# Projecting queries, keys and values of the second layer in blocks of 512 columns instead of 384

## The chip, the cores and the metric

The kernel runs on one core of one Trainium2 chip. Its time is the device time of one execution in microseconds, given as the median of a few runs. Five engines work side by side, each through its own list of instructions in order: TensorE (PE in the profile, with its weight loads as PEld), VectorE (DVE), ScalarE (ACT), GpSimd (POOL) and SyncE (SP), which issues nearly all of this kernel's transfers. Semaphores tie the lists together. Matmul results go to PSUM, from where DVE and ACT read them.

## The reference

Two layers work on 512 tokens of width 1024 with 16 heads of 64. Each layer does

```
hn = rms_norm(x, gain);  y = mixer(hn);  x = x + y
```

Layer A (dilated attention) projects to three groups of queries, keys and values and to a gate. Layer B (neighbourhood attention on a grid of 8 rows and 64 columns) is the one that the change touches:

```
proj = hn @ w_in                       # 1024 x 4096: q, k, v, gate
q = rms_norm(q per head, q_gain) / 8;  k = rms_norm(k per head, k_gain)
logits = q . k + bias(row, column),  masked to a window of 16 columns
y = softmax(logits) @ v * silu(gate);  return y @ w_out
```

All inputs and outputs are 32-bit floats.

## The kernel before

**Matmuls.** Each float is split into a rounded high part and a rest (`split`, line 124: ACT rounds at line 128, DVE or, two times in five, GpSimd subtracts at line 134). A product is then three matmuls: high by high, high by low, low by high (`mm3`, line 215). All matmuls are issued in `matmul` at line 209, all transposes on TensorE at line 213, so the profile tells them apart by their tiles: `acc<-` are projections and output products, `log` scores, `o` the weighted sum of values, `tp` transposes.

**Weights.** The weights lie in memory in the order in which they are used. `blocks` (line 137) lists the blocks, `loads` cuts them into transfers of at most 1024 columns, `raws` keeps three of those in flight in SBUF, and `splits` (line 186) splits pieces of 384 or 512 columns and runs three pieces ahead of the matmuls (line 192). `kernel`'s helper `_layout` packs the weights on the host in the same order.

**Layer B** works on eight pairs of heads, called `hc` 0 to 7. For each pair `main_b` (line 1000) does two things on TensorE:

- `project_qk(384, 4, "raw", hc, ...)`: queries, keys and values of the pair, 128 columns each. For each of eight slices of the width (`k`) and each of four groups of 128 tokens (`i`), one `mm3` with the normalised tokens as the stationary operand and 384 weight columns as the moving one, into four accumulators (`project`, line 245). After the last slice each accumulator is evacuated by ACT (line 477) into a part of the tile `rk`, and `squares` (line 278) forms the sums of squares of queries and keys: four heads' worth, GpSimd at line 284, DVE at line 285.
- `project_t`: the gate's 128 columns, now with the weights stationary and all 512 tokens moving, 24 matmuls. DVE multiplies the result by the token scale (line 1007), ACT takes the tanh, and DVE ends the SiLU later.

`head_norm` (line 291) turns the sums into factors with a Newton iteration for the inverse square root (`rsqrt`, line 105; on GpSimd it has 14 operations, on DVE 11) and multiplies them in on DVE (line 307). In layer B the multiplication is held back until the pair's gate has been scaled (`later`, line 1008).

**The attention of a pair** is `side_b` (line 1015): transposes of queries and keys, scores in two halves (`scores`), softmax on DVE and ACT, and the turning of the probabilities. For pairs 0 to 5 these are turned by DVE into the tile `tr` and sent through memory (`turner`, line 733: a write `td<-tr`, four reads `pt<-td`), and the weighted sum (`weigh`, line 1098) follows later. Pairs 6 and 7 turn them on TensorE. `put_y` (line 674) multiplies by the gate and splits the result for the output product.

**The order of the work.** The order on TensorE is written out by hand. `run` (line 906) walks through the main generator (projections, output product) and, in between, pulls steps from the side generator (the attentions) whenever its due time has come. Time here is a clock that the program itself keeps while it issues matmuls (line 207: 213 ns for a moving operand of 512 columns). `yield "wait", ("raw", hc), 12000` means: go on when 12 us of that clock have passed since block `hc` was projected. `later_on` sets a timer on the same clock. A guard such as `("qk", hc - 1)` makes the main generator pull side steps until that stamp exists. On the other engines a scheduler places the instructions by estimated times, except where `keep_in_program_order` fixes them.

The bias of a pair is loaded by `bias_b` (line 718) into one of two tiles; the gate tiles are three, the accumulators four, the side banks of PSUM four.

Of the kernel before, what the change touches and what calls it, by code (L numbers as in the profile page):

```python
# [13 lines left out]
F32 = mybir.dt.float32  # L14
# [8 lines left out]
P = 128  # L23
S = 512
D = 1024
DH = 64
NHC = 8
KT = 8
# [5 lines left out]
A_HC = 1280 * KT  # L34
A_OUT = A_HC * NHC
B_IN = A_OUT + KT * D
B_HC = 512 * KT
B_OUT = B_IN + B_HC * NHC
W_COLS = B_OUT + KT * D


@with_exitstack
def tile_hybrid_encoder(
# [93 lines left out]
    def blocks():  # L137

        for hc in range(NHC):
            b = hc * A_HC  # L140
            first = hc == NHC - 1
            yield from ((b + 512 * KT * (i ^ first), 512, KT) for i in range(2))
            if hc == NHC - 1:
                yield b - A_HC + 1152 * KT, 128, KT
            yield b + 1024 * KT, 128, KT
            if hc != NHC - 2:
                yield b + 1152 * KT, 128, KT
        yield from outs(A_OUT)
        for hc in range(NHC):
            b = B_IN + hc * B_HC  # L150
            yield from ((b, 384, KT), (b + 384 * KT, 128, KT))
        yield from outs(B_OUT)

    def outs(b):
# [133 lines left out]

    later = []

    def head_norm(raw, ss, ns, held, delay=0):


        rs = wk.tile([P, 32], F32, tag="rs", name="rs")
        rsqrt(nc.vector if ns == 8 else nc.gpsimd, rs[:, : 4 * ns], ss[:, : 4 * ns], 4 * ns, 1.0 / DH)

        def scale():
            for i in range(4):
                by = rs[:, i * ns : (i + 1) * ns].unsqueeze(2)
# [142 lines left out]
    def part(n):  # L442
        return rk[:, 1024 * n : 1024 * n + 1024].rearrange("p (i c) -> p i c", i=4)

    def project_qk(n, ns, key, hc, guard, first=False, **kw):

        box = []

        def evac(i, acc):
            if not box:  # L450
                if key == "rawq":
                    t = wk.tile([P, 4 * n], F32, tag="rawq", name=key, bufs=1)
                    box.append(
                        t.rearrange("p (c i r) -> p c i r", c=16, i=4)
                        if moved(hc)
                        else t.rearrange("p (i c) -> p i c", i=4)
                    )
                elif key == "rawk":
                    box.append(part(0))
                    st["v12", hc] = part(1 + hc % 3)  # L460
                else:
                    o = 4 * n * (hc % 3)
                    box.append(rk[:, o : o + 4 * n].rearrange("p (i c) -> p i c", i=4))
                box.append(wk.tile([P, 32], F32, tag="ss", name="ss"))
            raw, ss = box
            if key == "rawq" and moved(hc):
                src = acc.rearrange("p (f a r) -> p f a r", f=4, a=4)
                pieces = [(raw[:, :, i, :].rearrange("p (a f) r -> p f a r", a=4), src)]
            elif key == "rawk":
                pieces = [(raw[:, i, :], acc[:, :256]), (st["v12", hc][:, i, :], acc[:, 256:])]  # L470
            else:
                pieces = [(raw[:, i, :], acc[:, :n])]
            for dst, src in pieces:
                if first:
                    nc.scalar.copy(dst, src)
                else:
                    nc.scalar.activation(dst, src, AF.Copy, scale=rs_n[:, i : i + 1])  # L477
            if not first:
                squares(raw[:, :, i, :] if key == "rawq" and moved(hc) else raw[:, i, : ns * 64], ss, i, ns)

        tile_of = lambda hn: lambda k, i: hn[:, k, P * i : P * (i + 1)]
        yield from project(tile_of(hn_h), tile_of(hn_l), n, evac, guard, **kw)
        raw, ss = box
        if first:
            st["first"] = raw, ss
            return
        normed(raw, ss, ns, key, hc)

    def normed(raw, ss, ns, key, hc):
        head_norm(raw, ss, ns, key == "raw", 9000 if key == "rawk" and 0 < hc < NHC - 1 else 0)  # L490
        if key == "rawq" and moved(hc):
            turn_q(raw)
        st[key, hc] = raw
        stamp[key, hc] = clock[0]
# [502 lines left out]
        nc.vector.tensor_add(xk, xk, acc)  # L997
        nc.sync.dma_start(out[P * f : P * f + P, :], xk)

    def main_b(hc):  # L1000
        yield from project_qk(384, 4, "raw", hc, ("qk", hc - 1) if hc else ("rs", "b"))
        acc = []
        yield from project_t(acc)
        yield ("yb", hc - 3, "y") if hc else ("rs", "all")
        gt = wk.tile([P, S], F32, tag="gt", name="gt", bufs=3)
        eg = wk.tile([P, S], F32, tag="eg", name="eg")
        tc.keep_in_program_order(nc.vector.tensor_mul(gt, acc[0], rs_half))
        while later:
            later.pop()()
        nc.scalar.activation(eg, gt, AF.Tanh)  # L1010
        gated(hc, gt, eg)
# [2 lines left out]

    def side_b(hc):
        if hc >= 2 and far(hc - 2):
            yield "wait", ("raw", hc), 1500
            pending.pop(0)()
            yield
        if hc >= 1 and far(hc - 1):  # L1020
            if hc + 1 < NHC:
                st["e", hc + 1] = bias_b(hc + 1)
        yield "wait", ("raw", hc), 12000 if hc < NHC - 1 else 11000
        raw = st.pop(("raw", hc))
        e = st.pop(("e", hc))
        qh = wk.tile([P, 512], F32R, tag="q0h", name="qh", bufs=1)
# [70 lines left out]

        def weigh():
            assert not any(t.left for t in turners)
            o = bank("o")  # L1100
            mms = []


            for d, n, m, i, a in (
# [5 lines left out]
                if n == 256:  # L1110
                    q, p = [[P, 2]] + q, [[32, 2]] + p
                mms.append((
                    lambda t_, d=d, q=q: sb(t_, d, q),
                    lambda hs, m=m: raw[:, m, 256 + hs.start : 256 + hs.stop],
                    lambda hd, p=p, i=i, a=a: sb(pt, at(a, hd, i), p),
                ))
            side_by_side(o, mms)
# [22 lines left out]
    def main():  # L1140
# [5 lines left out]
        gap[0] = cycle((500, 500, 800))  # L1146
        for hc in range(2):
            st["e", hc] = bias_b(hc)
        for hc in range(NHC):
            yield from main_b(hc)  # L1150
        yield from out_product("yb", sink_b)

    def side():
# [83 lines left out]
def _layout(x, norm_gain, a_w_in, a_w_out, a_q_gain, a_k_gain, t5_bias,  # L1237
# [20 lines left out]
        parts.append(cols(wa, [c(0, 2)]))  # L1258
        parts.append(cols(wa, [9 * D + P * hc]))
    parts += outs(wao)  # L1260
    for hc in range(NHC):
        parts.append(cols(wb, [i * D + P * hc for i in range(3)]))
        parts.append(cols(wb, [3 * D + P * hc]))
    parts += outs(wbo)
    w = np.concatenate(parts, axis=1)

# [32 lines left out]
```

## Time and profile before

| what | value |
|---|---|
| runs of the kernel, median (lowest to highest) | 851.97 us (850.87 to 852.74), 3 runs |
| the profiled execution, its own time | 852.44 us |
| its span in the trace | 850.6 us |
| instructions | 15397 |
| granted TensorE clock, mean | 0.999 |
| memory read / written | 109.11 MB / 31.12 MB |

In the rows of the profile, a group's row has line, engine, operation, tiles, shapes and count, then its total busy time and the mean of one in ns, then the idle time ahead of it and what ended it. A row of the timeline begins with start and duration in us. A row of stretches has the busy time of each engine between two times. A row of waits says who waited for whom: total us, times, longest. Layer B's first projection starts at 577 us, its output product at about 793 us.

### The profile page before, as it was taken

The numbers are of one execution on the slowest core, as the hardware profiler recorded it, in microseconds if no ns is written. First come the engines' busy times: TensorE is split into PE (matmuls) and PEld (weight loads), VectorE is DVE, ScalarE is ACT, GpSimd is POOL, SyncE is SP. The second block draws the span as 40 slices with busy tenths as digits, with TensorE's granted clock in tenths as the row PEclk, the third lists the DMA queues.
The fourth block names the chain that finished last, engine by engine and source line by source line (L and its number), as shares of the span: only waits on it lengthen the run. The fifth ranks groups of instructions, "written<-read, shape, count | busy, mean of one in ns | idle before, by whom it ended". The sixth has DMA issues, their size and how long they took to land.

```text
span 850.6 us, 15397 instructions
## 1 busy us (share of the span) xinstructions
PE 842.8 (99%) x5546; PEld 702.5 (83%) x5546; DVE 518.5 (61%) x1336; ACT 431.5 (51%) x923; POOL 309.8 (36%) x494
## 2 busy tenths in 40 slices
PE   9999999999999999999999999999999999999998
PEld 7788878788788788788788787789998898889786
DVE  7354684684674674674675745447567656766642
ACT  7433653653653653652653554355366655665531
POOL 2252441542541541542531341121354335542511
PEclk9999999999999999999999999999999999999999
DMA  7346377477478378378375562264245664555333
GB/s 250 110 126 216 97 228 227 137 226 241 128 227 248 102 228 243 102 230 246 99 236 159 147 191 79 60 241 146 82 143 138 174 175 148 168 163 158 99 97 127
DMA packets 65228, 141.23 MB, mean 166 GB/s; under 512 B 5760, under 2 KB 23104, under 8 KB 65152
## 3 DMA queue, kind: packets, MB, share of 16 engines
q1 hardware_dynamic: 65008, 139.99, 54.5%
q8 instruction: 44, 0.72, 0.3%
q10 hardware_dynamic: 144, 0.26, 0.1%
q14 instruction: 32, 0.26, 0.1%
HBM read 109.11 MB, written 31.12 MB: 165 GB/s over the span
## 4 chain that ended last, share of the span: by engine, by line
PE 94%; ACT 3%; DVE 1%; DMA 1%; issue 0%; DVEq 0%; ACTq 0%
PE acc L209 80%; PE log L209 5%; PE o L209 5%; PE tp L213 3%; ACT p L1084 1%; ACT p L672 1%; DMA x_all<-in_xt 0%; ACT p L831 0%; ACT wh L128 0%; DVE hn_l L397 0%; ACT rawk L477 0%; DMA eb<-lb_d 0%; PE pa L209 0%; PE pl L209 0%; DVE p L820 0%
## 5 line engine op out<-in xcount | busy, mean ns | idle before, releaser
L128 ACT CAST wh<-wraw 128x512 fp32r<-128x512 f32 (+1 forms) x275 | 161.4, 588 | 294.7 <-PE acc L209 258.0
L209 PE MATMUL acc<-wh,hn_h 128*128 128x512 f32 (+1 forms) x768 | 293.8, 383 | 1.6 <-ACT rawq L477 0.8
L209 PE MATMUL acc<-wh,hn_l 128*128 128x512 f32 (+1 forms) x768 | 285.6, 373 | 0.0
L209 PE MATMUL acc<-wl,hn_h 128*128 128x512 f32 (+1 forms) x768 | 285.5, 373 | 0.0
L134 POOL TENSOR_TENSOR wl<-wraw,wh 128x512 fp32r<-128x512 f32 (+1 forms) x110 | 136.9, 1244 | 361.0 <-ACT wh L128 341.7
L134 DVE TENSOR_TENSOR wl<-wraw,wh 128x512 fp32r<-128x512 f32 (+1 forms) x166 | 111.1, 670 | 141.5 <-ACT wh L128 137.0
L209 PEld LDWEIGHTS acc<-wh,hn_h 128*128 128x128 f32 x768 | 144.6, 188 | 29.2 <-issue 4.9
L209 PEld LDWEIGHTS acc<-wh,hn_l 128*128 128x128 f32 x768 | 144.5, 188 | 20.8
L209 PEld LDWEIGHTS acc<-wl,hn_h 128*128 128x128 f32 x768 | 145.0, 189 | 18.9
L209 PE MATMUL acc<-y,wh 128*128 128x512 f32 x256 | 81.3, 399 | 0.0
L209 PE MATMUL acc<-hn_h,wh 128*128 128x512 f32 x192 | 77.1, 401 | 0.9 <-ACT rawq L477 0.6
L209 PE MATMUL acc<-hn_h,wl 128*128 128x512 f32 x192 | 74.9, 390 | 0.0
L209 PE MATMUL acc<-hn_l,wh 128*128 128x512 f32 x192 | 74.8, 390 | 0.0
L672 ACT ACTIVATE p<-p,mn 128x512 f32<-128x512 f32 (+3 forms) x128 | 69.3, 586 | 0.0
L831 ACT ACTIVATE p<-p,mn 128x512 f32<-128x512 f32 (+1 forms) x64 | 44.8, 701 | 44.7 <-DVE mn L820 44.5
L285 DVE TENSOR_REDUCE ss<-sq 128x4 f32<-128x256 f32 (+1 forms) x96 | 48.4, 505 | 31.2 <-POOL sq L284 19.7
L744 DVE STREAM_TRANSPOSE tr<-p 128x512 f32<-128x512 f32 (+1 forms) x80 | 53.7, 684 | 9.9 <-ACT p L672 9.5
L284 POOL TENSOR_TENSOR sq<-rawk 128x256 f32<-128x256 f32 x64 | 40.3, 637 | 48.2 <-ACT rawk L477 45.1
L209 PEld LDWEIGHTS acc<-y,wh 128*128 128x128 f32 x256 | 46.3, 188 | 10.2 <-issue 1.1
L209 PE MATMUL acc<-y,wl 128*128 128x512 f32 x128 | 50.0, 391 | 0.0
L209 PEld LDWEIGHTS acc<-hn_h,wh 128*128 128x128 f32 x192 | 36.1, 188 | 10.8 <-ACT rawk L477 2.1
L209 PEld LDWEIGHTS acc<-hn_h,wl 128*128 128x128 f32 x192 | 36.0, 188 | 7.8
(138 smaller groups left out, 1038.7 us busy)
## 6 DMA issues: line engine op xcount, KB each, us to landing
wraw<-in_w SPq DMA_DIRECT2D x95, 512.0 KB
wraw<-in_w SPq DMA_DIRECT2D x38, 384.0 KB
td<-tr SPq DMA_DIRECT2D x14, 1024.0 KB
pt<-td SPq DMA_DIRECT2D x56, 256.0 KB
qd<-rawq SPq DMA_DIRECT2D x6, 1024.0 KB
qt<-qd SPq DMA_DIRECT2D x24, 256.0 KB
td<-tr SPq DMA_DIRECT2D x6, 896.0 KB
pt<-td SPq DMA_DIRECT2D x24, 224.0 KB
```

The source lines that it names most:

```text
L128: nc.scalar.copy(h, raw)
L134: eng.tensor_sub(l, raw, h.bitcast(F32))
L209: nc.tensor.matmul(o, l, r, **kw)
L213: nc.tensor.transpose(o, i, ident)
L284: nc.gpsimd.tensor_mul(sq, v, v)
L285: nc.vector.tensor_reduce(ss[:, i * ns : (i + 1) * ns], sq.rearrange("p (a b) -> p a b", b=64), axis=AX.X, op=ALU.add)
L672: nc.scalar.activation(pr, pr, AF.Copy, scale=mn[:, 3:4])
L744: nc.vector.transpose(dst, src[:, :n].rearrange("p (i b k) -> p i b k", b=4, k=32))
L831: nc.scalar.activation(row, row, AF.Exp, bias=mn[:, 1:2], scale=-1.0, accum_out=mn[:, 2:3])
L1084: nc.scalar.activation(pr[:, o : o + n], pr[:, o : o + n], AF.Exp, bias=mn[:, 0:1], scale=-1.0, accum_out=mn[:, 2:3])
```

## The change

Layer B's weights are cut in another way. Six blocks of 512 columns take the place of the eight blocks of 384: four with the queries and keys of two pairs each (four heads: q, k of one pair, then q, k of the next), and two with the values of four pairs each (eight heads). The gate blocks stay as they are. The order of all blocks is a list, and the host packs the weights in that order.

- A query block evacuates into a tile of its own (`rawq`, one buffer), a value block into half of `rk`; value blocks have no sums of squares. `st["vb", n]` is where `weigh` now reads the values.
- The sums of squares of a query block's first pair are formed at each evacuation as before, those of the second pair after all four. The first pair's inverse square root is on DVE (`quick=True`), its multiplication held back for the gate in the second and fourth block; the second pair's is on GpSimd, with its multiplication set 9 us later by a timer.
- Both pairs of a block are stamped when the block ends, and the delays in `side_b` become lists by pair.
- The first query block is followed by a value block, and the third by a value block and the fourth query block, with no gate between; gates come two and two, and four in a row at the end.

The diff, without the parts in the host's packing that repeat the list:

```diff
+B_PARTS = (
+    ("qk", 0), ("v", 0), ("gate", 0), ("gate", 1), ("qk", 1), ("gate", 2), ("gate", 3),
+    ("qk", 2), ("v", 1), ("qk", 3), ("gate", 4), ("gate", 5), ("gate", 6), ("gate", 7),
+)
...
-        for hc in range(NHC):
-            b = B_IN + hc * B_HC
-            yield from ((b, 384, KT), (b + 384 * KT, 128, KT))
+        b = B_IN
+        for kind, _ in B_PARTS:
+            n = P if kind == "gate" else 512
+            yield b, n, KT
+            b += n * KT
...
-    def head_norm(raw, ss, ns, held, delay=0):
+    def head_norm(raw, ss, ns, held, delay=0, quick=False):
...
-        rsqrt(nc.vector if ns == 8 else nc.gpsimd, rs[:, : 4 * ns], ss[:, : 4 * ns], 4 * ns, 1.0 / DH)
+        rsqrt(nc.vector if ns == 8 or quick else nc.gpsimd, rs[:, : 4 * ns], ss[:, : 4 * ns], 4 * ns, 1.0 / DH)
...
+                elif key == "v":
+                    box.append(rk[:, 4 * n * hc : 4 * n * hc + 4 * n].rearrange("p (i c) -> p i c", i=4))
                 else:
-                    o = 4 * n * (hc % 3)
-                    box.append(rk[:, o : o + 4 * n].rearrange("p (i c) -> p i c", i=4))
-                box.append(wk.tile([P, 32], F32, tag="ss", name="ss"))
+                    t = wk.tile([P, 4 * n], F32, tag="rawq", name=key, bufs=1)
+                    box.append(t.rearrange("p (i c) -> p i c", i=4))
+                box.append(None if key == "v" else wk.tile([P, 32], F32, tag="ss", name="ss"))
...
-            if not first:
+            if not first and key != "v":
                 squares(raw[:, :, i, :] if key == "rawq" and moved(hc) else raw[:, i, : ns * 64], ss, i, ns)
...
+        if key == "v":
+            st["vb", hc] = raw
+            return
+        if key == "raw":
+            ss2 = wk.tile([P, 32], F32, tag="ss", name="ss")
+            for i in range(4):
+                squares(raw[:, i, 256:], ss2, i, 4)
+            head_norm(raw[:, :, :256], ss, 4, hc % 2 == 1, quick=True)
+            head_norm(raw[:, :, 256:], ss2, 4, False, 9000)
+            for n in range(2):
+                st[key, 2 * hc + n] = raw[:, :, 256 * n : 256 * n + 256]
+                stamp[key, 2 * hc + n] = clock[0]
+            return
...
-    def main_b(hc):
-        yield from project_qk(384, 4, "raw", hc, ("qk", hc - 1) if hc else ("rs", "b"))
+    def gate_b(hc):
...
-            yield "wait", ("raw", hc), 1500
+            yield "wait", ("raw", hc), (1500, 23500, 9500, 31000, 8000, 23000)[hc - 2]
...
-        yield "wait", ("raw", hc), 12000 if hc < NHC - 1 else 11000
+        yield "wait", ("raw", hc), (12000, 33000, 12000, 26000, 12000, 33500, 11000, 26000)[hc]
...
+            vb = st["vb", hc // 4]
...
-                    lambda hs, m=m: raw[:, m, 256 + hs.start : 256 + hs.stop],
+                    lambda hs, m=m: vb[:, m, P * (hc % 4) + hs.start : P * (hc % 4) + hs.stop],
...
-        for hc in range(NHC):
-            yield from main_b(hc)
+        for kind, i in B_PARTS:
+            if kind == "qk":
+                yield from project_qk(512, 4, "raw", i, ("qk", 2 * i - 1) if i else ("rs", "b"))
+            elif kind == "v":
+                yield from project_qk(512, 0, "v", i, None)
+            else:
+                yield from gate_b(i)
```

More of the change, by code (lines that the diff above doesn't have):

```diff
@@ L36 @@
 B_IN = A_OUT + KT * D
-B_HC = 512 * KT
-B_OUT = B_IN + B_HC * NHC
+B_PARTS = (
+    ("qk", 0), ("v", 0), ("gate", 0), ("gate", 1), ("qk", 1), ("gate", 2), ("gate", 3),
+    ("qk", 2), ("v", 1), ("qk", 3), ("gate", 4), ("gate", 5), ("gate", 6), ("gate", 7),
+)
+B_OUT = B_IN + 4 * KT * D
 W_COLS = B_OUT + KT * D
@@ L486, in project_qk @@
             return
+        if key == "v":
[11 more added lines that the diff above has]
+            return
         normed(raw, ss, ns, key, hc)
     def normed(raw, ss, ns, key, hc):
-        head_norm(raw, ss, ns, key == "raw", 9000 if key == "rawk" and 0 < hc < NHC - 1 else 0)
+        head_norm(raw, ss, ns, False, 9000 if key == "rawk" and 0 < hc < NHC - 1 else 0)
         if key == "rawq" and moved(hc):
@@ L1260, in _layout @@
     parts += outs(wao)
-    for hc in range(NHC):
-        parts.append(cols(wb, [i * D + P * hc for i in range(3)]))
-        parts.append(cols(wb, [3 * D + P * hc]))
+    for kind, i in B_PARTS:
+        if kind == "qk":
+            starts = [n * D + P * hc for hc in (2 * i, 2 * i + 1) for n in range(2)]
+        elif kind == "v":
+            starts = [2 * D + 512 * i + P * n for n in range(4)]
+        else:
+            starts = [3 * D + P * i]
+        parts.append(cols(wb, starts))
     parts += outs(wbo)
```

## The prediction, made before the result was known

> **What bounds the kernel.** First the page: engine totals, then the chain that ended last.
>
> ```profile
> PE 842.8 (99%) x5546; PEld 702.5 (83%) x5546; DVE 518.5 (61%) x1336; ACT 431.5 (51%) x923; POOL 309.8 (36%) x494
> ...
> PE 94%; ACT 3%; DVE 1%; DMA 1%; issue 0%; DVEq 0%; ACTq 0%
> ```
>
> TensorE is never without work for long, and it makes up 94% of the chain. So the time moves by what TensorE's own instructions take, and by the few places where it waits. The table of stretches, for layer B's projections and attention (from the first projection matmul to the middle of the output product) and for layer A:
>
> ```profile
> 577.20:818.70 241.50, 240.55 (x1523) 214.21 (x1521) 153.97 (x457) 138.28 (x359) 98.75 (x185) 1.00 0.47 139
> 34.90:574.60 539.70, 538.30 (x3762) 436.40 (x3762) 333.38 (x831) 266.63 (x516) 197.28 (x291) 1.00 0.59 177
> ```
>
> The columns are length, then busy time of PE, PEld, DVE, ACT and POOL, the granted clock (1.00 in both), the DMA share and GB/s. In layer B DVE is at 64%, ACT at 57%, POOL at 41%: none is a bound, but each can be late for a moment. "Busy" counts the tail of a pipelined matmul, so the waits inside those 240.55 us have to be read from start to start.
>
> **1. The columns.** Before, a block of 384 columns has 8 x 4 x 3 = 96 matmuls, eight blocks 768. After, six blocks of 512 columns have 576. The columns are the same, 294,912; only what is paid per instruction changes. Narrow ones in order of time: from the first row to the third stand 20 groups of three (the second row counts the group's first member), so 60 matmuls in 590.04 - 579.64 = 10.40 us, 173.3 ns each.
>
> ```profile
> 579.64 0.33 PE L209 MATMUL acc<-wh,hn_h 128*128 128x384 f32 x1
> ```
> ```profile
> L209 PE MATMUL acc<-wh,hn_h 128*128 128x384 f32 x20 | 6.7, 334 | 0.0
> ```
> ```profile
> 590.04 0.95 PE L209 MATMUL pk<-ones,ssq 128*128 128x1 f32 x8
> ```
>
> Wide ones in layer A, with the same kind of operands (the count is again of one in three): 36 in 264.76 - 256.60 = 8.16 us, 226.7 ns each.
>
> ```profile
> 256.60 0.39 PE L209 MATMUL acc<-wh,hn_h 128*128 128x512 f32 x1
> ...
> 264.76 0.60 PE L213 MATMUL tp<-ident,vt 128*128 128x128 f32 x4
> ```
> ```profile
> L209 PE MATMUL acc<-wh,hn_h 128*128 128x512 f32 x12 | 4.7, 389 | 0.0
> ```
>
> 128 columns more cost 53.4 ns, which leaves 13.2 ns that do not depend on the columns. 768 x 173.3 - 576 x 226.7 = 133.1 - 130.6 = **-2.5 us**; all of it is on TensorE, so on the path. The Trainium skill, "TensorE: Matmul & The Clock Gate", section "Back-to-back issue gap", puts the part per matmul at 2.5 ns at full clock, and by it the gain would be 192 x 2.5 = 0.5 us, an estimate; the two pitches here do not agree with that.
>
> **2. Evacuations.** The block after a projection writes its first accumulator again, so ScalarE must have emptied it (line 477).
>
> ```profile
> 594.96 0.33 PE L209 MATMUL acc<-wh,hn_l 128*128 128x384 f32 x1
> 595.13 0.39 PE L209 MATMUL acc<-hn_h,wh 128*128 128x512 f32 x1
> 595.36 0.40 PE L209 MATMUL acc<-hn_l,wh 128*128 128x512 f32 x1
> ...
> 621.17 0.34 PE L209 MATMUL acc<-wh,hn_l 128*128 128x384 f32 x1
> 621.62 0.50 PE L209 MATMUL acc<-hn_h,wh 128*128 128x512 f32 x1
> 621.96 0.39 PE L209 MATMUL acc<-hn_l,wh 128*128 128x512 f32 x1
> ...
> 702.20 0.34 PE L209 MATMUL acc<-wh,hn_l 128*128 128x384 f32 x1
> 702.51 0.50 PE L209 MATMUL acc<-hn_h,wh 128*128 128x512 f32 x1
> ```
> ```profile
> PEld acc L209 <- ACT rawk L477: 2.1, 6, 0.5
> ```
> ```profile
> 701.90 1.03 ACT L477 ACTIVATE rawk<-acc,rs_n 128x384 f32<-128x384 f32 x2
> ```
>
> Pair 0 (594.96) has no softmax beside it: the gate starts 0.17 us later, no wait. Pair 1 starts 0.45 us later, 0.28 too much, and its second matmul 0.34 later instead of 0.23: 0.39 lost. The waits of the weight loads count six such cases; at 702 it is 0.31, so 0.14 plus 0.11, 0.25 lost. Six cases at 0.25 to 0.39 are 1.5 to 2.3 us; I take 1.8. The cause is seen at 701.90: the first accumulator's last matmul started nine narrow ones before 702.20, at 700.64, and was done 0.33 later, about 701.0; ScalarE, busy with exponentials, came 0.9 us after that.
>
> ```profile
> L477 ACT ACTIVATE rawq<-acc,rs_n 128x512 f32<-128x512 f32 x32 | 21.5, 686 | 1.1 <-PE acc L209 1.1
> L477 ACT ACTIVATE rawk<-acc,rs_n 128x384 f32<-128x384 f32 x32 | 17.0, 567 | 0.3 <-DVE rs_n L116 0.3
> ```
>
> After the change nine matmuls of 226.7 follow the first accumulator, 2.0 us instead of 1.6, against an evacuation 0.12 us longer (686 against 567 ns). Also fewer blocks end beside a softmax. By the schedule's clock (a wide block is 20.5 us plus what is put into it) attention 0 has its last scores at 19 and the value block ends at 23; attention 3 has them at 33 and the third query block ends at 38. The other blocks end later behind them: the second value block 5 us, the fourth query block 8, the second 15; the first has none before it. I keep 0.4 us for the two or three close ones: **-1.4 us**. Ends: 0 and -2.3.
>
> **3. Three single waits.**
>
> ```profile
> 577.16 0.33 PE L209 MATMUL acc<-wh,hn_h 128*128 128x384 f32 x1
> ...
> 578.58 0.34 PE L209 MATMUL acc<-wh,hn_l 128*128 128x384 f32 x1
> 579.01 0.45 PE L209 MATMUL acc<-wh,hn_h 128*128 128x384 f32 x1
> ```
> ```profile
> 578.36 0.61 DVE pt L981
> ```
> ```profile
> 676.70 0.39 PE L209 MATMUL acc<-hn_h,wl 128*128 128x512 f32 x1
> 677.33 0.74 PE L209 MATMUL o<-pt,rawk 128*64 128x128 f32 x9 [0.25 <-DMA eb<-lb_d]
> ```
> ```profile
> 787.71 0.38 PE L213 MATMUL tp<-ident,p 128*128 128x128 f32 x2
> 788.45 0.33 PE L213 MATMUL tp<-ident,p 128*128 128x128 f32 x1 [0.36 <-ACT p L672]
> ```
>
> At the start of layer B the tenth matmul waits, 0.43 instead of 0.17, until DVE has added the last output tile of layer A (578.36 + 0.61 = 578.97). Wide matmuls reach that accumulator at 577.16 + 9 x 0.227 = 579.2, so this goes: -0.3. The weighted sum of pair 1 leaves TensorE 0.25 us without work, its probabilities just back from memory; after the change it is placed 23.5 us behind the second query block, some 17 us after those transfers: -0.25. Pair 6's third transpose starts 0.63 us after the second at 787.82, where 0.11 is usual, so it waits 0.5 us for ScalarE, which evacuates pair 7 between the softmax's parts; after the change that pair was evacuated with pair 6's block, more than 11 us earlier: -0.5. Together -1.05, **-1.1**, ends 0 and that.
>
> **4. What is added.** One query block holds two pairs, so its norms come in a burst.
>
> ```profile
> L284 POOL TENSOR_TENSOR sq<-rawk 128x256 f32<-128x256 f32 x64 | 40.3, 637 | 48.2 <-ACT rawk L477 45.1 <-DVE mn L671 0.8 <-ACT p L1084 0.3
> L115 DVE SCALAR_TENSOR_TENSOR na<-na,nv 128x32 f32<-128x32 f32 x24 | 6.7, 279 | 0.8
> L134 POOL TENSOR_TENSOR wl<-wraw,wh 128x512 fp32r<-128x512 f32 x11 | 14.4, 1305 | 63.6 <-ACT wh L128 56.7 <-DVE mn L1074 6.9
> ```
> ```profile
> 625.82 0.20 POOL L108 TENSOR_SCALAR nv<-ss 128x16 f32<-128x16 f32 x1
> ...
> 630.33 0.22 POOL L120 TENSOR_TENSOR rs<-rs,na 128x16 f32<-128x16 f32 x1
> ```
>
> GpSimd has eight squares (5.1 us) and one chain of 14 small operations (630.55 - 625.82 = 4.7); DVE takes the other chain, 11 operations at 0.28 or less, 3.1 us. Four times each. What hides it: weights are split three steps ahead (line 192), 3 x 12 x 0.227 = 8.2 us, more than before (6.2). The number of splits falls from 80 to 64, 40 weight transfers become 32 of the same bytes, and 32 evacuations become 24; the first chain of a pair moves from GpSimd to DVE, 19 us less there. Weight DMAs keep their order on SP's queue; the bias loads and the transposing round trips are issued later against the weights, with the same counts. Four gates in a row take turns on four accumulators and three gate tiles, whose earlier uses end before. Attentions 2 and 3 start 14 us apart instead of a block and a gate, with one transposing tile between them; what waits there is DVE, and behind it splits that have the 8 us. Layer A's wide blocks (1.4 us idle in 539.7) are the nearest row, hence near nothing: **+0.5**, between 0 and the 11.6 of the first rival. Nothing in the layout on the host or in the tail of the output product (last matmul, add, store) changes.
>
> **Sum.** -2.5 - 1.4 - 1.1 + 0.5 = -4.5. The profiled execution took 852.44 us, 1.8 more than its span and 0.5 over the median of 851.97. 852.44 - 4.5 = **847.9**.
>
> **Rivals.**
> (a) *Splits starve, slower.* If GpSimd runs its whole burst ahead of a split, that split is late by 5.1 + 4.7 + 1.3 - 8.2 = 2.9 us at each of four query blocks, 11.6 in all: 847.9 - 0.5 + 11.6 = 859.0. It decides once a split lies over 8.2 us behind its cast. For it: small GpSimd operations stretch beside DVE,
>
> ```profile
> 627.79 0.22 POOL L113 TENSOR_TENSOR na<-rs 128x16 f32<-128x16 f32 x1
> 628.08 0.56 POOL L118 TENSOR_TENSOR na<-na,nv 128x16 f32<-128x16 f32 x1
> ```
> ```profile
> 628.01 0.55 DVE L134 TENSOR_TENSOR wl<-wraw,wh 128x384 fp32r<-128x384 f32 x1
> ```
>
> 0.56 instead of 0.22, while DVE subtracted one tile from another. The Trainium skill, "GPSIMD Engine Reference", section "1. Specifications", says that its SBUF interfaces are shared with VectorE, with contention when that has two SBUF inputs; the row agrees. Against it: GpSimd is 41% busy, and its splits mostly wait for casts (56.7 of 63.6 us above). Chance 0.12.
> (b) *Wide matmuls pay more in layer B.* Six gate matmuls from 595.13 to the next instruction take 230 ns each;
>
> ```profile
> 596.51 1.06 PE L209 MATMUL pa<-ident,rs_n 128*128 128x128 f32 x8
> ```
>
> (596.51 - 595.13) / 6; 576 x 3.3 = 1.9 us of the gain goes: 849.8. For it: that stretch. Against it: it lies right after a change of operands. A part per matmul of a few ns, so a gain of 0.5 for 2.5 us, would give 849.9, and both pitches speak against that. The Trainium skill's "TensorE: Matmul & The Clock Gate", in the section named above, would have it so. Chance 0.14, of which 0.02 for this last.
> (c) *New boundaries wait.* Value and query blocks follow one another without a gate between, gates come in rows. Ten of fourteen boundaries at pair 1's 0.39 are 3.9 against the 0.4 kept: 851.4. For it: the evacuation behind exponentials above. Against it: longer cover and fewer softmaxes. Chance 0.14.
>
> **Chances and range.** The forecast, 846.2 to 849.4, has 0.60: its lower end takes 2.3 for the evacuations and nothing for the burst (846.4, and the spread of runs), its upper end none of the evacuation gain. A difference under 0.2% (1.7 us) cannot be told from none. Faster, under 850.3: 0.60 + 0.12 from (b) + 0.02 from (c) = 0.74. Within: 0.02 + 0.10 and 0.01 of a weak (a), 0.13. Slower: 0.11 of (a) and 0.02 of (c), 0.13. The range, 846.2 to 852.5, holds the forecast, (b) and nearly all of (c), and leaves out (a) and the little below.
>
> **What would show it.** Right: the projection groups with 128x512 alone, starts 227 ns apart in the six blocks; weight loads waiting for line 477 under 1 us in all; layer B about 4.5 us shorter, other stages as before; GpSimd's splits before the second chain of each block. Wrong: weight loads idle behind line 134, or starts of 230 ns and more, or line 477 in the chain at the end of each block; above all, any TensorE wait of over 1 us in the 10 us behind a query block.

## The result, and the profile after

The kernel with blocks of 512 columns takes **856.52 us**, the median of six runs (854.83 to 858.44); the kernel before took 852.36 in the same comparison (850.87 to 853.47, six runs). The ratio is 1.0052, 95% interval 1.0038 to 1.0067: slower, where 847.9 was forecast. The profiled execution took 858.42 us, that of before 852.44. Lines have moved in the file: matmuls are line 215 (209), evacuations 485 (477), splits 138 (134), the scale's multiplication 313 (307), the gate's multiplication 1028 (1007).

The page of the kernel after, the same lines that were shown of before (span first):

```profile
span 856.6 us, 14911 instructions
...
PE 843.6 (98%) x5354; PEld 678.0 (79%) x5354; DVE 527.7 (62%) x1370; ACT 428.4 (50%) x899; POOL 293.1 (34%) x432
...
PE 87%; DVE 4%; ACT 3%; DMA 2%; POOL 1%; issue 1%; SPq 1%; POOLq 0%; ACTq 0%; DVEq 0%
```

TensorE has 192 instructions less, yet only 87% of the chain is its own (94% before). DVE and GpSimd now stand in it: TensorE waited for them. Where layer B begins, the timeline of the kernel after has

```profile
577.23 0.39 PE L215 MATMUL acc<-wh,hn_h 128*128 128x512 f32 x1
```

against 577.16 before. So nothing was lost ahead of layer B. From there to the end of the span it is 856.6 - 577.2 = 279.4 us, before 850.6 - 577.2 = 273.4: the 6 us are all behind this point. TensorE's waits there, in the view of waits from 570 to 830 us:

```profile
PE log L215 <- DVE kl L665: 2.6, 1, 2.6
PE acc L215 <- DVE gt L1028: 2.1, 1, 2.1
PE o L215 <- DMA pt<-td: 1.0, 1, 1.0
PE acc L215 <- ACT rawk L485: 0.3, 1, 0.3
PE acc L215 <- ACT raw L485: 0.3, 1, 0.3
PE acc L215 <- DVE pt L1003: 0.2, 1, 0.2
```

Before, this view had two rows, 0.4 and 0.2 us in all. The two waits over 2 us are for DVE. The first one, in the timeline of TensorE:

```profile
677.45 0.40 PE L215 MATMUL acc<-wh,hn_l 128*128 128x512 f32 x1
679.92 0.51 PE L215 MATMUL acc<-wh,hn_h 128*128 128x512 f32 x1 [2.07 <-DVE gt L1028]
```

The third query block has begun; three of its accumulators are free, the fourth still holds the gate of pair 3. Start to start it is 2.47 us where 0.23 is usual: 2.24 lost. DVE at the same time, and the chain of the same kernel:

```profile
677.83 1.43 DVE L313 TENSOR_TENSOR raw<-raw,rs 128x256 f32<-128x256 f32 x4 [3.32 <-POOL rs L124]
679.18 0.69 DVE L1028 TENSOR_TENSOR gt<-acc,rs_half 128x512 f32<-128x512 f32 x1
```
```profile
675.77 1.24 POOL wl L138
...
677.57 0.23 POOL rs L124
```

The second pair's multiplication (line 313, the one that the timer sets at 9 us) comes next in DVE's list. It needs factors that GpSimd has not finished: its chain of 14 operations runs from 671.90 to 677.79, and a split of 1.24 us was put into it. DVE stands idle for 3.32 us, and the gate's multiplication, which is ready and would free the accumulator, stands behind. The second wait, TensorE and DVE:

```profile
782.44 0.38 PE L215 MATMUL log<-kh,qh 64*128 64x256 f32 x2
785.40 0.58 PE L215 MATMUL log<-kl,qh 64*128 64x256 f32 x2 [2.58 <-DVE kl L665]
...
787.35 0.63 PE L215 MATMUL acc<-hn_l,wh 128*128 128x512 f32 x1
787.78 0.63 PE L215 MATMUL acc<-hn_h,wl 128*128 128x512 f32 x1
...
791.19 0.59 PE L215 MATMUL acc<-hn_h,wh 128*128 128x512 f32 x1
```
```profile
782.17 2.50 DVE L313 TENSOR_TENSOR raw<-raw,rs 128x256 f32<-128x256 f32 x4 [0.71 <-POOL rs L124]
784.60 0.74 DVE L665 SCALAR_TENSOR_TENSOR kl<-tp,gk,kh 128x512 fp32r<-128x512 f32 x1
```

Here the four multiplications for pair 7 run just ahead of the low part of pair 6's keys, for which the scores on TensorE wait: 2.96 us start to start where 0.22 is usual, 2.74 lost. They take 2.50 us, at the first place 1.43. There GpSimd was idle beside them; here it does a split, from 782.39 for 1.33 us. In e1 below they take the same 2.50 beside a split, in e2 1.43 without one. Then something comes that layer B before, with its clock of 1.00, does not have: matmuls of 512 columns 0.43 us apart (787.35 to 787.78), nearly twice the usual 0.227, until 791. The granted clock in stretches of the same execution (length, busy times, then the clock):

```profile
784.40:784.80 0.40, 0.00 (x0) 0.00 (x0) 0.40 (x2) 0.00 (x0) 0.00 (x0) 0.74 0.88 343
784.80:791.20 6.40, 5.80 (x29) 4.32 (x29) 3.18 (x14) 3.43 (x12) 0.00 (x0) 0.50 0.59 134
791.20:791.60 0.40, 0.40 (x3) 0.38 (x2) 0.19 (x1) 0.40 (x3) 0.00 (x0) 0.73 0.00 0
```

The clock fell to 0.50 during the wait and stayed there for 6.8 us. So in this execution a wait of 2.7 us was also followed by a slow stretch. It does not come each time: of the six executions three had a mean granted clock of 0.996 or 0.997 (858.42, 858.44 and 854.83 us) and three of 0.999 or 1.0 (856.26 to 856.65 us). The median lies among the latter three, so the change is slower than the kernel before even without the slow stretch.

### The profile page after: what moved, and what is told of

Same layout as the page of the kernel before. It is cut to its first block, busy times and chain, and to the rows that moved or that the text cites. A ratio compares the mean times of both kernels' runs of the same rounds, so it can differ in the third digit from the quotient of the medians.

```text
span 856.6 us, 14911 instructions
## 1 busy us (share of the span) xinstructions
PE 843.6 (98%) x5354; PEld 678.0 (79%) x5354; DVE 527.7 (62%) x1370; ACT 428.4 (50%) x899; POOL 293.1 (34%) x432
## 4 chain that ended last, share of the span: by engine, by line
PE 87%; DVE 4%; ACT 3%; DMA 2%; POOL 1%; issue 1%; SPq 1%; POOLq 0%; ACTq 0%; DVEq 0%
PE acc L215 73%; PE log L215 5%; PE o L215 5%; PE tp L219 3%; DMA pt<-td 2%; ACT p L694 1%; DVE raw L313 1%; ACT p L1105 1%; DVE hn_l L403 1%; ACT p L853 0%; DMA x_all<-in_xt 0%; ACT raw L485 0%; DVE wl L138 0%; DVE ss L291 0%; ACT wh L132 0%
## 5 line engine op out<-in xcount | busy, mean ns | idle before, releaser
L132 ACT CAST wh<-wraw 128x512 fp32r<-128x512 f32 (+1 forms) x259 | 158.5, 613 | 295.1 <-PE acc L215 254.0
L215 PE MATMUL acc<-wh,hn_h 128*128 128x512 f32 x704 | 283.8, 404 | 4.2 <-DVE gt L1028 2.1
L215 PE MATMUL acc<-wl,hn_h 128*128 128x512 f32 x704 | 274.9, 391 | 0.0
L215 PE MATMUL acc<-wh,hn_l 128*128 128x512 f32 x704 | 274.7, 391 | 0.0
L138 POOL TENSOR_TENSOR wl<-wraw,wh 128x512 fp32r<-128x512 f32 (+1 forms) x104 | 134.8, 1296 | 379.2 <-ACT wh L132 356.0
L215 PEld LDWEIGHTS acc<-wh,hn_h 128*128 128x128 f32 x704 | 132.6, 188 | 40.7 <-issue 5.4
L215 PEld LDWEIGHTS acc<-wh,hn_l 128*128 128x128 f32 x704 | 132.6, 188 | 28.9
L215 PEld LDWEIGHTS acc<-wl,hn_h 128*128 128x128 f32 x704 | 133.0, 189 | 25.0
L215 PEld LDWEIGHTS acc<-hn_l,wh 128*128 128x128 f32 x192 | 36.4, 190 | 7.1
```

Of the source, the lines that this page charges most:

```text
L132: nc.scalar.copy(h, raw)
L138: eng.tensor_sub(l, raw, h.bitcast(F32))
L215: nc.tensor.matmul(o, l, r, **kw)
```

## The experiments

Three theories for the two waits over 2 us. **Order (O):** the second pair's multiplication stands at a bad place in DVE's list, ahead of instructions for which TensorE waits; it costs what it does wherever its factors come from. **GpSimd (Q):** DVE waits for factors, and the burst of norms on GpSimd makes them late; with the chain taken off GpSimd the loss goes. **Load (L):** DVE simply has too much to do in these stretches, and no order helps. Beside them, **the rest (E2, first called E):** the boundary waits and the late transfer, each at most 1.0 us in the view of waits. In the forecasts of e1 to e4 the first two are still one theory, called Q: DVE waits for GpSimd, and what TensorE needs stands behind. Order as a theory of its own was written down after e1, with e5.

**e1: the second pair's factors on DVE too.**

```diff
-            head_norm(raw[:, :, 256:], ss2, 4, False, 9000)
+            head_norm(raw[:, :, 256:], ss2, 4, False, 9000, quick=True)
```

> The second pair's inverse square root runs on DVE too. Theory Q (blocked queue: DVE, in order, waits at line 313 for GpSimd's second chain, and the gate's multiplication and the keys' subtraction stand behind it): TensorE's waits of 2.2 us at 677 and 2.8 us at 782 go, and with the second one the half clock behind it; 856.5 falls to 849 to 851.5. Rival L (load: DVE and GpSimd simply have too much to do behind a query block): DVE gets 3 us more per block, so no gain or a loss, 856 to 858. Rival E (evacuations and late transfers at the new boundaries make the loss): under 1 us of gain, 855.5 or more.

Measured: 856.96 us (854.87 to 857.14, 5 runs), ratio to before 1.0051 [1.0037, 1.0064], as the change itself. DVE's timeline at the first place, and its multiplications at the second:

```profile
675.46 1.43 DVE L313 TENSOR_TENSOR raw<-raw,rs 128x256 f32<-128x256 f32 x4
676.81 0.69 DVE L1028 TENSOR_TENSOR gt<-acc,rs_half 128x512 f32<-128x512 f32 x1
...
780.88 2.50 DVE L313 TENSOR_TENSOR raw<-raw,rs 128x256 f32<-128x256 f32 x4
```

No idle time stands in these rows: DVE does not wait for GpSimd any more, and the gate and the keys still come behind the four multiplications; the waits for `gt` and `kl` are 1.7 and 2.6 us in this kernel. Theory Q, which had 849 to 851.5, falls. Order, load and the rest all fit.

At the first place this needs a reservation: e1 also puts the eleven operations of the second chain on DVE ahead of the multiplication. In the change DVE was idle from 674.51. With the factors ready then, the four multiplications (1.43) and the gate's (0.69) would have ended at about 676.6, an estimate from these rows, and TensorE needs the accumulator at about 677.7. So there the late factors and the order make the wait together. At the second place DVE waited 0.71 us for GpSimd, so with the factors ready some 1.9 of the 2.6 us would stay (an estimate likewise): there it is the order.

**e2: the second pair's multiplication later, the same work.**

```diff
-            head_norm(raw[:, :, 256:], ss2, 4, False, 9000)
+            head_norm(raw[:, :, 256:], ss2, 4, False, 20000)
```

> No work moves to another engine: the second pair's multiplication is only set 20 us behind its block instead of 9. Theory Q: the same two waits go, since GpSimd's chain is done 15 us behind the block; 848.5 to 851. Rival L: the same work in the same burst, 855 to 857. Rival E: 855.5 or more.

Measured: **850.31 us** (849.52 to 852.58, 11 runs), ratio 0.9982 [0.9972, 0.9992]: 6.2 us less than the change, with one number altered, and no work added or taken away. DVE's list now has the gate and the keys first:

```profile
675.59 0.69 DVE L1028 TENSOR_TENSOR gt<-acc,rs_half 128x512 f32<-128x512 f32 x1 [0.94 <-PE acc L215]
...
780.86 0.75 DVE L665 SCALAR_TENSOR_TENSOR kl<-tp,gk,kh 128x512 fp32r<-128x512 f32 x1 [0.68 <-ACT kh L661]
```

The gate's multiplication waits for its matmuls, and the keys for ScalarE: each starts when its data are there. The factors come no sooner than in the change: GpSimd's second chain at the first place ends at 678.38 here, there at 677.79. So a later place is enough, whatever makes the factors late. Load (855 to 857) and the rest (855.5 or more) fall. The same stretch of TensorE shows what the half clock had cost:

```profile
781.67 0.38 PE L215 MATMUL log<-kl,qh 64*128 64x256 f32 x2
...
784.94 0.50 PE L215 MATMUL acc<-hn_h,wh 128*128 128x512 f32 x1
```

From the second group of scores to the first gate matmul behind the second half, the same instructions take 784.94 - 781.67 = 3.27 us here and 791.19 - 785.40 = 5.79 in the change: 2.5 us from the clock alone. What is left in e2's view of waits is one of 1.5 us, for `pt<-td`, and four of 0.2 to 0.3.

**e3 and e4: each half alone.** The delay of 20 us only in the second query block (e3) or only in the fourth (e4).

```diff
-            head_norm(raw[:, :, 256:], ss2, 4, False, 9000)
+            head_norm(raw[:, :, 256:], ss2, 4, False, 20000 if hc == 1 else 9000)
```

> The later multiplication in the second query block alone. Theory Q: only the wait of 2.2 us at 677 goes, 853.5 to 855; the wait at 782 and the clock's fall behind it stay. Rivals L and E: 856 to 857.

> The later multiplication in the fourth query block alone. Theory Q: the wait of 2.8 us at 782 goes, and the matmuls at half clock behind it; 851 to 853.5, the granted clock 0.999 or 1.0 in every run; the wait at 677 stays. If the clock's fall has another cause than that wait, 853.5 and runs at 0.996 remain. Rivals L and E: 856 to 857.

Measured: e3 854.71 us (852.03 to 855.82, 12 runs), ratio 1.0028 [1.0018, 1.0038]; e4 853.46 us (851.29 to 854.56, 12 runs), ratio 1.0014 [1.0004, 1.0023]. Both medians lie in the ranges that theory Q, as it was then, gave for them. Each takes away its own wait and leaves the other. Against the change that is 1.8 and 3.1 us, against e2 4.4 and 3.2 too much: both halves are needed. The two gains sum to 4.9 and not to 6.2. In 11 of 12 executions of e3 and in 3 of 12 of e4 the mean granted clock was 0.997 to 0.998, in all of e2 at least 0.999; so it seems that either wait can be followed by a slow stretch, and not in each execution. For e4 a clock of 0.999 or more had been expected every time; its three slower executions left no trace, so that their slow stretch followed the wait at 677 is inferred. The profiled execution of e3 had none:

```profile
781.63 0.39 PE L215 MATMUL log<-kl,qh 64*128 64x256 f32 x2 [1.97 <-DVE kl L665]
...
782.75 0.40 PE L215 MATMUL acc<-hn_l,wh 128*128 128x512 f32 x1
782.99 0.40 PE L215 MATMUL acc<-hn_h,wl 128*128 128x512 f32 x1
```

After 1.97 us of idleness matmuls follow 0.24 us apart.

**e5: a delay for each block.** In e2, the transposes of pair 3 waited at 692 us, since 20 us put the multiplication behind a softmax on DVE.

```diff
-            head_norm(raw[:, :, 256:], ss2, 4, False, 9000)
+            head_norm(raw[:, :, 256:], ss2, 4, False, (9000, 15500, 9000, 20000)[hc])
```

> Theory O (order: what costs is where the second pair's multiplication stands in DVE's list, wherever its factors come from): set 15.5 us behind the second query block and 20 us behind the fourth, 9 behind the others, it stands behind the gate's multiplication and the keys' subtraction, and ahead of the softmax whose work delayed it by 0.7 us at 692 when it was set at 20. 849.5 to 850.5, with no TensorE wait on line 313 or 1028. Rival L (load of the burst): as at 20 us or slower, 850 to 852.

Measured: 850.23 us (849.49 to 851.9, 11 runs), ratio 0.9983 [0.9973, 0.9992]. The wait for line 313 is gone from the view of waits; in the median this cannot be told from e2. In this form the multiplication of blocks 0 and 2 is at 9 us again, so it was only the second and the fourth block that hurt.

**e8: the first pair's factors back on GpSimd** (on e5). It asks whether the other choice of the change, the chain on DVE, was worth its place there.

```diff
-            head_norm(raw[:, :, :256], ss, 4, hc % 2 == 1, quick=True)
+            head_norm(raw[:, :, :256], ss, 4, hc % 2 == 1)
```

> The fitted multiplications, but the first pair's inverse square root on GpSimd again, as in the kernel before. If the burst's place on the engines matters, GpSimd's two chains of 5 us in a row make the first pair's factors late for its transposes 12 us behind the block: waits of 1 to 3 us at pairs 2, 4 and 6, 852 to 858, and with them a clock under 0.999. Rival L, if DVE's 3 us per block are what hurts: 848 to 849.5.

Measured: 856.59 us (854.46 to 858.96, 6 runs), ratio 1.0058 [1.004, 1.0075]. The transposes of pairs 2, 4 and 6 now wait for the scaled queries (they lose about 0.8, 0.7 and 2.9 us), in its timeline of TensorE for pair 6 so:

```profile
778.02 1.01 PE L219 MATMUL tp<-ident,raw 128*128 128x128 f32 x3 [0.90 <-DVE raw L313]
```

The clock under 0.999 that was expected with it came in two of six executions. So the first pair does need the fast chain; the second, with 20 us to spare, does not (e2 has it on GpSimd).

**e6 and e7: the rest.** The wait for `pt<-td` in the chain of the change:

```profile
711.03 0.71 DVE wl L138
711.76 0.33 SPq L184
...
713.55 6.37 DMA pt<-td
719.97 1.75 PE o L215 x24
```

SP had to wait for a split before it could issue a weight load, and the reads of the turned probabilities stood behind that load; they landed at 713.55 + 6.37 = 719.92, 1.0 us late for the weighted sum of pair 2, by the view of waits. Of the way there 6.37 us are the reads themselves; whether they could be shorter is not tested. e6 puts that sum 4.5 us later and attention 4 (that of pair 4) 7.5 us later, e7 attention 3 and the sum of pair 1 as well. Both stand on e5; "put" is the list of delays of the weighted sums, "attention" that of line 1044.

```diff
-put        (1500, 23500, 9500, 31000, 8000, 23000)
+put        (1500, 23500, 14000, 31000, 8000, 23000)     # e6
+put        (1500, 30500, 14000, 31000, 8000, 23000)     # e7
-attention  (12000, 33000, 12000, 26000, 12000, 33500, 11000, 26000)
+attention  (12000, 33000, 12000, 26000, 19500, 33500, 11000, 26000)   # e6
+attention  (12000, 33000, 12000, 33500, 19500, 33500, 11000, 26000)   # e7
```

> On top of that the weighted sum of pair 2 at 14 instead of 9.5 us and attention 4 at 19.5 instead of 12 us behind the third query block. Theory E2 (the rest of the loss is two late evacuations of 0.6 us and one late transfer of probabilities, 1.1 to 1.6 us): the transfer's wait at 718 and the evacuation's at 738 go, 2.0 us less than the kernel with the fitted multiplication, 847.5 to 848.8. If the waits only move to the next thing in line, 849 to 850.5.

> On top of that attention 3 at 33.5 instead of 26 us and the weighted sum of pair 1 at 30.5 instead of 23.5 us behind the second query block, so that its exponentials come behind the third block's evacuations. Theory E2: the wait at 708 goes too, 0.6 us less, 847 to 848.3, near the predicted 847.9. If the exponentials of attentions 3 and 4 now crowd the value block, no gain: 848 to 850.

Measured: e6 850.04 us (848.29 to 850.87, 11 runs), ratio 0.9972 [0.9962, 0.9982]; e7 849.78 us (847.67 to 850.16, 10 runs), ratio 0.9968 [0.9956, 0.9979]. In e6 the wait at pair 2's sum and one of the two boundary waits go, in e7 the other. But a wait of 1.1 us for `pt<-td` stands in e6 at pair 4's sum, and 1.6 in e7: what is moved there makes the next transfer late. In e7 the keys of pair 3 are 0.4 late besides. Less came of it than the waits that went, 0.2 and 0.3 us in the medians, below what these runs can tell apart. Theory E2 had 847.5 to 848.8 and 847 to 848.3, so it missed twice, and what was written for waits that only move came out. The medians also hold a part that has nothing to do with these edits: layer B's first matmul starts at 575.35 us in the profiled execution of e3 and at 577.80 in that of e6. From there to the end of the span, one execution each, e5 takes 272.1 us, e6 and e7 270.8.

**e9: attention 6 and the sum of pair 4 later too** (and attention 3 and the sum of pair 1 1.5 us sooner than in e7).

```diff
-put        (1500, 30500, 14000, 31000, 8000, 23000)
+put        (1500, 29000, 14000, 31000, 13000, 23000)
-attention  (12000, 33000, 12000, 33500, 19500, 33500, 11000, 26000)
+attention  (12000, 33000, 12000, 32000, 19500, 33500, 15000, 26000)
```

> The fitted multiplications and attentions 3, 4 late, with two corrections: attention 3 at 32 instead of 33.5 us, so that the guard of the third query block no longer pulls its key transposes forward (0.7 us of waiting at 700), and the weighted sum of pair 4 at 13 instead of 8 us behind the fourth block with attention 6 at 15 instead of 11 (1.8 us of waiting for probabilities at 766). Theory E2: both go, some 2 us under the kernel before them: 847 to 848.3. If the waits move on to attention 6 and 7 and the output product: 849 to 851.

Measured: 851.34 us (850.7 to 853.19, 11 runs), ratio 0.9998 [0.9989, 1.0007]: a miss, above both ranges. The waits at which it aimed are gone, and a new one is there, with the same face as the first of the change (TensorE, then DVE):

```profile
786.51 0.60 PE L219 MATMUL tp<-ident,p 128*128 128x128 f32 x4
789.75 0.73 PE L215 MATMUL acc<-y,wh 128*128 128x512 f32 x2 [2.64 <-DVE gt L1028]
```
```profile
788.89 0.22 DVE L693 RECIPROCAL mn<-mn 128x1 f32<-128x1 f32 x2
789.02 0.67 DVE L1028 TENSOR_TENSOR gt<-acc,rs_half 128x512 f32<-128x512 f32 x1
```

Now pair 6's softmax stands ahead of a late gate's multiplication on DVE, and the output product waits for the accumulator. Behind it the clock falls again (last section).

**e10: the later attentions without the later multiplication** (e9 with 9000 in all blocks).

> The same, but the second pair's multiplication 9 us behind every block again, as in the changed kernel. Theory O: the gate's multiplication of the fourth gate waits behind it again, 2.2 us of TensorE near 677, and the clock falls in some runs; the keys of pair 6 now come behind it, so the 2.8 us near 782 do not return: 849.5 to 851. If the later attentions alone had made the gain: 847 to 848.5.

Measured: 855.56 us (854.43 to 857.23, 6 runs), ratio 1.0045 [1.0031, 1.0058]. The attentions' places alone bring 1.0 us against the change, which the two intervals do not tell from nothing; the multiplication's place brings 4.2, between e10 and e9. That too is a miss: theory O had 849.5 to 851 for it. The wait of 2.1 us at 677 came back as expected, but the keys of pair 6, which were to be clear of the multiplication, cost 1.2 and 0.3 us of waiting and were followed by a half clock (last section), and the output product waits 1.8 (2.6 in e9). The sign of the theory held, the size did not.

**e11: between e7 and e9.** The weighted sum of pair 4 at 10 us and attention 6 at 12.

```diff
-put        (1500, 29000, 14000, 31000, 13000, 23000)
+put        (1500, 29000, 14000, 31000, 10000, 23000)
-attention  (12000, 33000, 12000, 32000, 19500, 33500, 15000, 26000)
+attention  (12000, 33000, 12000, 32000, 19500, 33500, 12000, 26000)
```

> As the kernel of e9, with the weighted sum of pair 4 and the sixth attention put 3 us earlier (10000 and 12000 in place of 13000 and 15000). If what e9 lost came from the sixth attention's softmax standing ahead of gate 7's multiplication in DVE's list: the 2.8 us wait before the output product is gone or under 0.7 us, no half clock at 791, and the time is 847.5 to 849.0. If the wait only moves (to the weighted sum of pair 4 at about 766, or stays at the output product): 849.5 to 851.5. Over 852 neither holds.

Measured: **847.65 us** (846.88 to 848.78, 5 runs), before 850.8 beside it; ratio 0.9961 [0.9947, 0.9975]. It beats both kernels. Its view of TensorE's waits from 570 to 830 us has one row, the 0.2 us for `pt` at the start, and its granted clock was 1.0 in all five executions. The page and the first matmul of layer B are these:

```profile
span 845.1 us, 14912 instructions
```
```profile
576.44 0.39 PE L215 MATMUL acc<-wh,hn_h 128*128 128x512 f32 x1
```

Layer B takes 845.1 - 576.4 = 268.7 us, 4.7 less than before and 10.7 less than in the change as it was made, in one profiled execution each; between the medians of e11 and of before beside it lie 3.1 us.

## Why the prediction was wrong, point by point

**Step 1, the columns (-2.5): right.** In the first query block after, twenty matmuls start in 594.03 - 589.49 = 4.54 us, 227 ns each:

```profile
589.49 0.39 PE L215 MATMUL acc<-wh,hn_h 128*128 128x512 f32 x1
...
594.03 0.39 PE L215 MATMUL acc<-wh,hn_l 128*128 128x512 f32 x1
```

From 577 to 792 us one matmul of 512 columns into an accumulator follows another 712 times (projections and gates), in 660 of them after 0.22 to 0.24 us, so the other blocks are alike. Rival (b), wide matmuls that pay more, is refuted by it.

**Step 2, the evacuations (-1.4): the sign right, the rest too small.** I kept 0.4 us for boundaries beside a softmax. Two of them, at the ends of the third query block and of the second value block, have all of it. At the first (TensorE's timeline),

```profile
709.86 0.40 PE L215 MATMUL acc<-wh,hn_l 128*128 128x512 f32 x1
710.54 0.50 PE L215 MATMUL acc<-wh,hn_h 128*128 128x512 f32 x1 [0.29 <-ACT raw L485]
```

it is 0.68 us from start to start, 0.45 too much, for an evacuation that ScalarE did between exponentials, and 0.15 was lost one group of tokens earlier; the second boundary loses 0.6 in the same way. The two together are 1.2 us; by the prediction's own count, in which the second matmul's 0.34 us (710.54 to 710.88) instead of 0.23 is lost as well, four times here, they are 1.6 instead of 0.4. I had set both blocks down as 5 us clear of the attentions ahead of them. Rival (c) is thereby right in kind, at four tenths of its price of 3.9.

**Step 3, the single waits (-1.1): two of three.** The waits at pair 1's weighted sum and at pair 6's transposes are gone. The one at the start stayed:

```profile
579.60 0.50 PE L215 MATMUL acc<-wh,hn_h 128*128 128x512 f32 x1 [0.17 <-DVE pt L1003]
```
```profile
578.88 0.67 DVE L1003 TENSOR_TENSOR pt<-pt,acc 128x512 f32<-128x512 f32 x1
```

The tenth matmul was due at 577.23 + 9 x 0.227 = 579.27 and came at 579.60: 0.3 lost, as before. I had moved TensorE's instruction and left DVE's addition where it was; it moved as well, by 0.6 us in the timelines (578.27 before, 578.88 after). And a new wait of 1.0 us came, for the transfer of pair 2's probabilities. I had named that "the transposing round trips are issued later against the weights, with the same counts", and looked at counts, not at what SP waits for between them.

**Step 4, what is added (+0.5): this step failed.** I counted what the burst of norms costs on GpSimd and DVE, and asked only whether it makes the splits late, which have 8 us to spare. They are not late: no TensorE wait in the view above is for a split, and rival (a) did not come. But the burst ends in a multiplication on DVE, four instructions of 0.36 us or more, set by a timer that knows nothing of its factors or of what is queued behind it. I never named what stands behind that instruction in DVE's list. It was the gate's multiplication in one place and the keys in the other, and both are what TensorE waits for next. The price was 2.24 at 677 us, 2.74 at 782 and 2.5 from the clock behind it, 7.5 us instead of 0.5 in the profiled execution; in one without the slow stretch it would be the first two, 5.0. The prediction has no term for the clock at all. I took layer A's wide blocks for the nearest row; but there the norms of one block come in one piece, so they could not show this.

**Sum.** The profiled execution came out 858.4 - 847.9 = 10.5 us above the forecast, the median 8.6. Step 4 is 7.0 of the 10.5, the late transfer 1.0, the boundaries 1.2 and the start 0.3; together 9.5. The remaining 1.0 us I cannot place: layer B began at the same time as before, so they lie in it, in pieces too small for the view of waits. With all these waits but the start's taken away (e11), layer B is 4.7 us shorter than before, where the forecast had 4.5: a gain of the promised size can be had, and the change's own delays had hidden it. That the two numbers agree so well is partly luck: e11 has other places for six delays of the attentions besides, no late evacuation at all, and still the wait at the start; and the kernel before was not tuned again.

**The sign to look for** was right in kind and too narrow. "Any TensorE wait of over 1 us in the 10 us behind a query block" would have missed both. The second and the fourth query block end with these evacuations,

```profile
660.54 2.73 ACT L485 ACTIVATE raw<-acc,rs_n 128x512 f32<-128x512 f32 x4
...
763.60 2.39 ACT L485 ACTIVATE raw<-acc,rs_n 128x512 f32<-128x512 f32 x4
```

and the waits came at 677.45 and 782.44, 14 and 16 us after them: a delay of 9 us was in between.

**What is shown and what is argued.** That a later place of the multiplication on DVE removes the two waits is shown by e2, e3 and e4. That it does not help to take the second chain off GpSimd is shown by e1; what the late factors add to the waits of the change is an estimate from its rows, much of the first and at most 0.7 us of the second. That the half clock follows from the waits is read from its coming behind them in four traces and from its absence in e2 and e11; no run isolates it. That the late transfer comes from SP's order is read from the chain; e6 moved the weighted sum and not SP's list, so it shows only that the sum came too early for the transfer.

## What to carry to other kernels

When a change brings work in bursts to an engine that is not the bottleneck, list what stands behind the burst in that engine's in-order list and ask who waits for it; 62% busy says nothing on that. A deferred instruction should stand behind whatever frees an accumulator or feeds the next matmul, and as late as its own reader allows: here the same multiplications cost 6.2 us when set 9 us behind their block, and at 20 us one wait of 0.3. And when a schedule with delays written by hand is regrouped, the delays belong to the old grouping: try them anew before judging the regrouping.

## What the runs showed of the hardware that was not expected

A TensorE wait can cost more than its length. In the change the granted clock was 0.50 from about 784.59 to 791.42 us: 0.26 of the first of the three stretches quoted above is 0.21 us of half clock, 0.27 of the third 0.22, and with the 6.40 between them that is 6.8 us. It began while TensorE was still idle, 1.8 us after its last matmul was done (782.44 + 0.38). In e9 the wait was as long (2.64 us), but TensorE had been working again for 1.1 us when the clock fell:

```profile
790.80:791.20 0.40, 0.40 (x3) 0.30 (x2) 0.00 (x0) 0.39 (x1) 0.00 (x0) 0.58 0.00 0
791.20:794.00 2.80, 2.80 (x10) 2.31 (x9) 1.38 (x2) 0.00 (x0) 0.00 (x0) 0.50 0.00 0
794.00:794.40 0.40, 0.40 (x2) 0.29 (x2) 0.00 (x0) 0.00 (x0) 0.00 (x0) 0.66 0.00 0
```

By the same working 0.34 + 2.80 + 0.27 = 3.4 us, half of the 6.8. In e10 two shorter waits at 784 us, 1.20 and 0.33, came ahead of it:

```profile
786.00:789.00 3.00, 3.00 (x16) 2.14 (x16) 1.76 (x12) 2.80 (x11) 0.00 (x0) 0.56 0.02 5
789.00:792.00 3.00, 3.00 (x17) 2.36 (x14) 2.25 (x13) 2.51 (x9) 0.00 (x0) 0.87 0.00 0
```

The clock missing there, 0.44 and 0.13 of 3.00 us each, is 2.64 + 0.78 = 3.4 us of half clock again, and 3.4 by the same working in e1 behind its wait of 2.60. Waits of 2.07 us (the change at 677) and 1.97 (e3) had no such stretch in the profiled executions. So the length of a wait alone does not decide. The Trainium skill, "TensorE: Matmul & The Clock Gate", section "What's actually happening", says that the clock is set by activity in windows of about 3.4 us that run freely, whatever the kernel does. The lengths of 3.4 (three times) and 6.8 us agree with one and two such windows, and so does the start at no fixed distance from the wait. The Trainium skill has the clock fall after an idle window of that length; here a wait of 2.6 us was enough, and in e10 two that make 1.5, and the measurement decides. A rule for how much idleness a window takes is not settled by these runs.
